# Log-sum-exp over 16384 rows: sixteen loads cut inside the rows, and the last row's raw test ahead of the last range check

## The chip, the core, the metric

One core of a Trainium2 chip runs one program. The metric is device time in microseconds (us) of that core. Most runs of one program agree within 0.3%. "Faster" or "slower" needs 2%, which is 3.3 us here.

## The reference

```python
x = randn(32, 512, 1024).astype(float32)          # 16384 rows of 1024
max_x = max(x, axis=-1, keepdims=True)
out = max_x.squeeze(-1) + log(sum(exp(x - max_x), axis=-1))
```

## The kernel before

The 16384 rows lie over 128 partitions, 128 rows each ("row" below means one row in each of the 128 partitions, 512 KB in all). The kernel doesn't subtract the maximum. It takes exp of the raw data on ScalarE, sums on VectorE or in ScalarE's accumulator, takes the logarithm, and then checks that all sums lie within safe bounds; if any doesn't, a second, safe pass is run under a branch. So the fast path ends twice: with the landing of the last store, and with the branch that skips the second pass.

The rows come in loads into a ring of 48 slots. Each load is worked in pieces. "R" is one exp and one reduce over s rows; "T" is one exp and, per row, one VectorE instruction that adds its two halves with an accumulator; "A" is one exp with ScalarE's own accumulator, for one row.

```python
RING = 48
loads = [
    "R6 R5 R5", "R6 R5 R5", "R8 R8", "R8 R4 R4", "R4 R4 R3 R3 A A", "R6 T3 A A A", "R6 A A",
    "R2 A A T2", "R3 R3", "R3", "A A A", "T2 A", "T2", "T2", "T1", "A", "A",
]
...
    dma = nc.sync.dma_start(out=ring[:, p : p + size, :], in_=source(c, size)).ins
    for how, s in ops:
        v = ring[:, p : p + s, :]
        if how == "A":   exp = nc.scalar.activation(out=o, in_=v, func=AF.Exp, accum_out=sums)
        else:            exp = nc.scalar.activation(out=v, in_=v, func=AF.Exp)
        ...
    if c == LATE:        # 118 rows done: early Ln of 112 rows, early range check
        ...
nc.scalar.activation(out=res[:, W:NC], in_=sumexp[:, W:NC], func=AF.Ln)      # the last 16 rows
nc.sync.dma_start(out=out_rows, in_=res[:, 0:W])
last_store = nc.sync.dma_start(out=out_rest, in_=res[:, W:NC]).ins

check(LATE, LAST, 1)                                       # range check of rows 118 to 126
nc.vector.reduce_max(out=bad[:, 3:4], in_=last_row[:, 0, 0 : d // 16], axis=AX.X)   # raw test,
nc.vector.tensor_scalar(out=bad[:, 2:3], in0=bad[:, 3:4], scalar1=LOG_LOW, ...)     # last row
nc.tensor.matmul(count, lhsT=bad[:, 2:3], rhs=far, start=False, stop=False)
nc.tensor.matmul(count, lhsT=sumexp[:, LAST:NC], rhs=ones, start=False, stop=True)
nc.vector.tensor_scalar(out=fine, in0=count, scalar1=HIGH, scalar2=None, op0=ALU.is_lt)
...                                                        # branch on `fine`
```

`check` is two VectorE instructions (clamp; count what the clamp changed) and a matmul. "Truth value" below means the last instruction shown, `fine`. The "raw test" asks in each partition whether the largest of the first 64 raw values of the last row lies below `LOG_LOW` (the sum could then be too small); it needs the loaded row only, not its exp.

## Time and profile before

| | before |
|---|---|
| time | 163.57 us, median of 3 runs (163.52 to 163.73) |
| span in the trace | 161.76 us |
| busy share of the load queue | 97.0% |
| VectorE, ScalarE busy | 73%, 72% |
| first load landed, last load landed | 21.79, 157.95 |
| last exp, last store issued, landed | 157.98, 159.40, 160.99 |
| truth value; end of SyncE's waits other than for the store | 159.40; 160.55 |

The prediction shows the page's slices, the timeline of ScalarE's waits and the tail, and reads them. Landing times to two decimals are the semaphore events in the trace; where a fence can show them, they are ScalarE's start less 0.02.

### The profile page before, as it was taken

The numbers are of one execution on the slowest core, as the hardware profiler recorded it, in microseconds if no ns is written. First come the engines' busy times: TensorE is split into PE (matmuls) and PEld (weight loads), VectorE is DVE, ScalarE is ACT, GpSimd is POOL, SyncE is SP. The second block draws the span as 40 slices with busy tenths as digits, with TensorE's granted clock in tenths as the row PEclk, the third lists the DMA queues.
The fourth block names the chain that finished last, engine by engine and source line by source line (L and its number), as shares of the span: only waits on it lengthen the run. The fifth ranks groups of instructions, "written<-read, shape, count | busy, mean of one in ns | idle before, by whom it ended". The sixth has DMA issues, their size and how long they took to land.

```text
span 161.8 us, 221 instructions
## 1 busy us (share of the span) xinstructions
PE 0.8 (0%) x8; PEld 0.3 (0%) x8; DVE 118.5 (73%) x56; ACT 117.2 (72%) x60; POOL 0.2 (0%) x4
## 2 busy tenths in 40 slices
PE   0000000000000000000000000000000000000001
PEld 0000000000000000000000000000000000000000
DVE  0000002999959997299995999999999589799772
ACT  3000069980899609994299924999999999999994
POOL 0000000000000000000000000000000000000000
DMA  7996996997997997998898899889999999999990
GB/s 259 519 519 276 502 519 292 486 519 324 454 519 324 454 519 340 438 519 389 389 519 389 389 519 389 389 389 502 405 389 434 474 389 432 416 428 415 418 368 6
DMA packets 2738, 67.19 MB, mean 415 GB/s; under 512 B 560, under 2 KB 560, under 8 KB 944
## 3 DMA queue, kind: packets, MB, share of 16 engines
q1 hardware_dynamic: 2736, 67.18, 97.0%
q14 instruction: 2, 0.02, 0.0%
HBM read 67.11 MB, written 0.07 MB: 415 GB/s over the span
## 4 chain that ended last, share of the span: by engine, by line
DMA 53%; DVE 35%; ACT 10%; issue 1%; PE 0%
DMA ring<-in_x_dram 53%; DVE sumexp L132 35%; ACT ring L122 9%; ACT ring L120 1%; ACT last_exp L120 0%; PE count L202 0%; DVE fine L203 0%
## 5 line engine op out<-in xcount | busy, mean ns | idle before, releaser
L132 DVE TENSOR_REDUCE sumexp<-ring 128x3 f32<-128x3072 f32 (+5 forms) x21 | 109.5, 5276 | 37.2 <-ACT ring L122 37.2
L122 ACT ACTIVATE ring<-ring 128x3072 f32<-128x3072 f32 (+6 forms) x27 | 100.3, 3763 | 41.4 <-DMA ring<-in_x_dram 41.3
L120 ACT ACTIVATE ring<-ring 128x1024 f32<-128x1024 f32 x14 | 14.6, 1040 | 0.0
L137 DVE SCALAR_TENSOR_TENSOR ring<-ring 128x512 f32<-128x512 f32 x12 | 7.7, 687 | 2.1 <-ACT ring L122 2.1
L120 ACT ACTIVATION_READ_ACCUMULATOR ring<-ring 128x1 f32 x14 | 2.6, 187 | 0.0
L75 ACT ACT_TABLE_LOAD x1 | 1.3, 1283 | 0.8 <-PEq L264 0.8
L102 PE MATMUL count<-far,bad 128*1 128x1 f32 x4 | 0.4, 164 | 158.3 <-DVE clamped L98 158.3
L120 ACT ACTIVATE last_exp<-ring 128x1024 f32<-128x1024 f32 x1 | 1.0, 1027 | 0.0
L137 DVE DVE_READ_ACCUMULATOR ring<-ring 128x1 f32 x12 | 1.0, 83 | 0.0
L76 DVE MEMSET ones<- 128x1 f32 x1 | 0.1, 59 | 0.9 <-PEq L264 0.9
L203 DVE TENSOR_SCALAR fine<-count 1x1 int32<-1x1 f32 x1 | 0.1, 145 | 0.6 <-PE count L202 0.6
L94 DVE TENSOR_SCALAR clamped<-sumexp 128x118 f32<-128x118 f32 (+1 forms) x2 | 0.4, 197 | 0.2
L102 PEld LDWEIGHTS count<-far,bad 128*1 128x1 f32 x4 | 0.2, 81 | 158.4 <-DVE clamped L98 158.4
L98 DVE SCALAR_TENSOR_TENSOR clamped<-clamped,sumexp 128x118 f32<-128x118 f32 (+1 forms) x2 | 0.5, 225 | 0.1
L155 ACT ACTIVATE res<-sumexp 128x112 f32<-128x112 f32 x1 | 0.3, 280 | 0.0
L190 ACT ACTIVATE res<-sumexp 128x16 f32<-128x16 f32 x1 | 0.2, 216 | 0.0
L197 DVE TENSOR_REDUCE bad<-ring 128x1 f32<-128x64 f32 x1 | 0.2, 220 | 0.0
L201 PE MATMUL count<-far,bad 128*1 128x1 f32 x2 | 0.2, 164 | 0.2 <-DVE bad L198 0.2
L202 PE MATMUL count<-ones,sumexp 128*1 128x1 f32 x2 | 0.2, 164 | 0.1
L120 ACT ACTIVATION_READ_ACCUMULATOR last_exp<-ring 128x1 f32 x1 | 0.2, 187 | 0.0
L198 DVE TENSOR_SCALAR bad<-bad 128x1 f32<-128x1 f32 x1 | 0.2, 154 | 0.0
L98 DVE DVE_READ_ACCUMULATOR clamped<-clamped,sumexp 128x1 f32 x2 | 0.2, 82 | 0.0
(7 smaller groups left out, 0.6 us busy)
## 6 DMA issues: line engine op xcount, KB each, us to landing
ring<-in_x_dram SPq DMA_DIRECT2D x1, 6144.0 KB, 28.8
ring<-in_x_dram SPq DMA_DIRECT2D x2, 3072.0 KB, 27.9
ring<-in_x_dram SPq DMA_DIRECT2D x3, 1536.0 KB, 29.2
ring<-in_x_dram SPq DMA_DIRECT2D x1, 4096.0 KB, 27.8
ring<-in_x_dram SPq DMA_DIRECT2D x2, 1024.0 KB, 30.0
ring<-in_x_dram SPq DMA_DIRECT2D x3, 512.0 KB, 25.9
ring<-in_x_dram SPq DMA_DIRECT2D x5, 35.3
out_dram<-res SPq DMA_DIRECT2D x1, 56.0 KB, 8.7
```

The source lines that it names most:

```text
L75: nc.scalar.preload_act_table_set("natural_log_exp_and_others")
L94: nc.vector.tensor_scalar(out=clamped[:, c0:c1], in0=sumexp[:, c0:c1], scalar1=LOW, scalar2=HIGH, op0=ALU.max, op1=ALU.min,)
L98: counted = nc.vector.scalar_tensor_tensor(out=clamped[:, c0:c1], in0=clamped[:, c0:c1], scalar=0.0, in1=sumexp[:, c0:c1], op0=ALU.bypass, ...
L102: nc.tensor.matmul(count, lhsT=bad[:, i : i + 1], rhs=far, start=i == 0, stop=False)
L120: exp = nc.scalar.activation(out=o, in_=v, func=AF.Exp, accum_out=sums)
L122: exp = nc.scalar.activation(out=v, in_=v, func=AF.Exp)
L132: added = [nc.vector.reduce_sum(out=sums, in_=v, axis=AX.X)]
L137: nc.vector.scalar_tensor_tensor(out=lo, in0=lo, scalar=1.0, in1=ring[:, p + r, H:d], op0=ALU.mult, op1=ALU.add, accum_out=sums[:, r : r + 1],
L155: ln = nc.scalar.activation(out=res[:, 0:W], in_=sumexp[:, 0:W], func=AF.Ln)
L190: nc.scalar.activation(out=res[:, W:NC], in_=sumexp[:, W:NC], func=AF.Ln)
L197: nc.vector.reduce_max(out=bad[:, 3:4], in_=last_row[:, 0, 0 : d // 16], axis=AX.X)
L198: nc.vector.tensor_scalar(out=bad[:, 2:3], in0=bad[:, 3:4], scalar1=LOG_LOW, scalar2=None, op0=ALU.is_lt)
```

## The change

Its intent: one load fewer, and late loads sized so that ScalarE keeps up with them, by letting a load end inside a row (13.5, 12.5, 7.5, 5.5, 3.5, 2.75, 2.25, 1.5 rows; exp takes what has landed, the sums only whole rows). On VectorE, the raw test of the last row moves ahead of the last range check. Core of the diff (the ring becomes two-dimensional and positions are counted in elements; that and the second pass are cut):

```diff
+    x_rows = x_flat[0 : P * W].rearrange("(p c) d -> p (c d)", p=P)
     loads = [
-        "R6 R5 R5", "R6 R5 R5", "R8 R8", "R8 R4 R4", "R4 R4 R3 R3 A A", "R6 T3 A A A", "R6 A A",
-        "R2 A A T2", "R3 R3", "R3", "A A A", "T2 A", "T2", "T2", "T1", "A", "A",
+        (16, "R8 R7 A"), (16, "R8 R7 T1"), (16, "R8 R8"), (16, "R6 R5 R5"), (13.5, "R5 R4 T4"),
+        (12.5, "R7 R6"), (9, "A A A A A A A A A"), (7.5, "R3 R2 R2"), (5.5, "R4 T2"),
+        (4, "A A A A"), (3.5, "T3"), (2.75, "T3"), (2.25, "T2"), (1.5, "T2"), (1, "A"), (1, "A"),
     ]
-    LATE = 118
+    LATE = 119
...
+                upto = end if k + 1 == len(ops) else p + s * d
+                v = ring[:, here:upto]
                 exp = nc.scalar.activation(out=v, in_=v, func=AF.Exp)
...
-    check(LATE, LAST, 1)
-    nc.vector.reduce_max(out=bad[:, 3:4], in_=last_row[:, 0, 0 : d // 16], axis=AX.X)
-    nc.vector.tensor_scalar(
+    seen = nc.vector.reduce_max(out=bad[:, 3:4], in_=last_row[:, 0 : d // 16], axis=AX.X)
+    low = nc.vector.tensor_scalar(
         out=bad[:, 2:3], in0=bad[:, 3:4], scalar1=LOG_LOW, scalar2=None, op0=ALU.is_lt
     )
+    first, _ = check(LATE, LAST, 1)
+    in_this_order(add, seen)
+    in_this_order(low, first)
```

## The prediction

> **What bounds the kernel now.** I read the page's DMA slices first, then the chain of waits, then the timeline of the last 5 us, and last the landing events of the loads.
>
> The slices of the page (40 of 4.04 us each; busy tenths of the DMA engines, then GB/s) and its queue table:
>
> ```profile
> DMA  7996996997997997998898899889999999999990
> ...
> q1 hardware_dynamic: 2736, 67.18, 97.0%
> ```
>
> The load queue holds 97.0% of 16 engines' span, and the only weak slices are the first and the last. (The sixes and sevens in between are big packets counted whole in the slice where they start.) The input is 67.11 MB, every byte of it is read once before and after, and no slice in the middle is empty: transfers bound this kernel, and the time is one start, one stream, one tail.
>
> The list of ScalarE's waits in the timeline gives the pace of the stream, because ScalarE stands idle until each of the early loads lands (start us, us busy, engine, line; in brackets the idle time before and what ended it):
>
> ```profile
> 21.81 14.04 ACT L122 ACTIVATE ring<-ring 128x6144 f32<-128x6144 f32 x3 [19.74 <-DMA ring<-in_x_dram]
> ...
> 41.15 14.04 ACT L122 ACTIVATE ring<-ring 128x6144 f32<-128x6144 f32 x3 [5.30 <-DMA ring<-in_x_dram]
> ...
> 60.50 13.95 ACT L122 ACTIVATE ring<-ring 128x8192 f32<-128x8192 f32 x2 [5.31 <-DMA ring<-in_x_dram]
> ...
> 79.86 14.04 ACT L122 ACTIVATE ring<-ring 128x8192 f32<-128x8192 f32 x3 [5.41 <-DMA ring<-in_x_dram]
> ...
> 99.21 12.43 ACT L122 ACTIVATE ring<-ring 128x4096 f32<-128x4096 f32 x4 [5.31 <-DMA ring<-in_x_dram]
> ...
> 138.08 8.07 ACT L122 ACTIVATE ring<-ring 128x3072 f32<-128x3072 f32 x3 [0.28 <-DMA ring<-in_x_dram]
> ```
>
> A load of 16 rows per partition (64 KB each) takes 19.34 to 19.36 us. From 99.21 to 138.08, 32 rows came in four loads (12, 8, 6, 6) in 38.87 us; two loads of 16 would take 38.70. Two more loads cost 0.17, so a load costs about 0.08 by itself and a row about 1.204. The landing events confirm it: loads of 12, 8, 6, 3, 2 and 1 rows are 14.53, 9.72, 7.31, 3.69, 2.49 and 1.28 us apart, which 0.079 + 1.2045 per row gives within 0.01. The last row lands at 157.95 (the page: issued at 138.07, landed 19.9 later).
>
> The tail, from the timeline of the last 5 us:
>
> ```profile
> 156.88 1.04 ACT L120 ACTIVATE ring<-ring 128x1024 f32<-128x1024 f32 x1
> 157.29 0.08 DVE L137 DVE_READ_ACCUMULATOR ring<-ring 128x1 f32 x1
> 157.29 0.69 DVE L137 SCALAR_TENSOR_TENSOR ring<-ring 128x512 f32<-128x512 f32 x1
> 157.83 0.19 ACT L120 ACTIVATION_READ_ACCUMULATOR ring<-ring 128x1 f32 x1
> 157.90 0.08 DVE L137 DVE_READ_ACCUMULATOR ring<-ring 128x1 f32 x1
> 157.98 1.03 ACT L120 ACTIVATE last_exp<-ring 128x1024 f32<-128x1024 f32 x1
> 158.09 0.17 DVE L94 TENSOR_SCALAR clamped<-sumexp 128x9 f32<-128x9 f32 x1
> ...
> 159.16 0.22 ACT L190 ACTIVATE res<-sumexp 128x16 f32<-128x16 f32 x1
> ...
> 159.40 0.34 SPq L192 DMA_DIRECT2D out_dram<-res  x1
> 159.40 0.14 DVE L203 TENSOR_SCALAR fine<-count 1x1 int32<-1x1 f32 x1 [0.59 <-PE count L202]
> ```
>
> The last exp starts at 157.98. Elsewhere the next exp follows the start of an accumulator read after 0.09, so ScalarE was ready at 157.83 + 0.09 = 157.92: it waited 0.06, for the landing at 157.95 and the 0.02 to 0.03 that every release takes here. So the load sets the end, but ScalarE is only 0.06 behind; the chain of waits, which sees no gap worth counting, puts that step down to ScalarE. From the last exp the rest is a fixed tail: 0.96 to the accumulator read, 0.22 to the Ln, 0.24 to the store's issue, 1.59 to its landing (160.99), 0.77 of closing barriers to 161.76. The timed value is 163.57, the span 161.8.
>
> **What the Trainium skill says.** "DMA: Bandwidth & Descriptors", Queues, rings and completion order: on each engine descriptors are consumed in ring order. The trace agrees: loads land in order, evenly, with up to eight queued, so a fixed completion cost is hidden except for the last load. The same page, Anatomy of one DMA, puts a fixed cost of about 2.0 us on a DMA issued by another path; here, in a full queue, the trace shows 0.08. The same page, How a descriptor splits into AXI transactions: a descriptor that doesn't start on a multiple of 256 B costs extra beats. The new loads start and end on quarter rows, multiples of 1024 B, so none should; no run before shows it for such sizes. "ScalarE: Activation LUTs", What ACT_TABLE_LOAD costs: 186 ns + 0.833 per element, consecutive instructions overlapping by 93 ns. The trace agrees: 1040 ns for 1024 elements, 7025 for 8192, pairs overlapping by 96.
>
> **The change part by part.** *Removed:* one load (17 to 16), 0.079 us of the stream. *Moved:* the cuts. The first four loads stay 16 rows, so the first landing (21.79) and the pace to 79.84 stay. Bytes are the same. With 0.079 + 1.2045 n, landings after 79.84 are: 13.5 rows 96.18, 12.5 at 111.31, 9 at 122.23, 7.5 at 131.35, 5.5 at 138.05, 4 at 142.95, 3.5 at 147.24, 2.75 at 150.63, 2.25 at 153.42, 1.5 at 155.31, 1 at 156.59, 1 at 157.87. That is 157.95 - 0.08.
>
> *Is the queue still fed?* A load of the second lap may go out when the slots it overwrites have been summed. VectorE needs 140 + 1068 ns per row for a reduce (3345 at 3 rows, 8682 at 8). The first load's sums end at about 45.0, the second's at 65, the third's at 84.8, the fourth's at 102.5, the 13.5-row load's at 114.7, the 12.5-row load's at 131.1. The stream needs load 4 queued by about 58, load 5 by 77, load 6 by 94, load 7 by 109, load 8 (slots of the fourth and the fifth: 108) by 120, load 12 (slots of the sixth: 124.6) by 145. More than 10 us to spare each time: nothing starves.
>
> *ScalarE at the end.* Step from start to start: 0.09 + 0.855 per row, and 1.037 for a row with its accumulator read. From the landing at 122.23: nine such rows to 131.58; 7.5 rows in three pieces to 138.26; 5.5 in two to 143.14; four rows to 147.29; 3.5 rows to 150.37 and the early Ln (0.19) to 150.56. It then waits for the landings at 150.63 (done 153.09) and 153.42 (start 153.44): 2.25 rows to 155.45, 1.5 to 156.83, a row to 157.86. The last row is released at 157.89. ScalarE is ready 0.03 before: again a near tie, 0.09 earlier than now.
>
> *VectorE.* The last pair sum follows the 1.5-row exp, which ends about 156.92: two rows of 0.615 to 158.17. The raw test (steps 0.25 and 0.20) needs only the loaded row, then the range check (0.21, and 0.23 to the PE) ends at about 159.05. The PE still takes the range check's matmul first, in program order, so the three products end at about 159.5 instead of 159.38 and the truth value comes at about 159.57 instead of 159.40. That isn't on the path: the last store lands at about 160.9, and the branch's end, which SyncE saw at 160.37 before, may come at 160.5 unnoticed. The swap is worth 0.
>
> Sum: 0.079 less for the load, 0 for the cuts while their rates hold, 0 for the swap: 163.57 - 0.08 = 163.49.
>
> **The rivals.** (1) Sizes that aren't whole rows cost the transfers something. Eight loads have such sizes, and an engine carries 8 packets of each (128 partitions over 16 engines). With 20 ns more per packet, my guess of a bad case, that is 8 x 8 x 0.02 = 1.3 us: 164.8. Against it: packets have followed size in a straight line so far (161 ns at 4 KB, 912 at 24 KB, 2415 at 64 KB). (2) ScalarE becomes the bound of the tail. Its slack is 0.03, and after the landing at 153.42 it has 4.42 us of work for 4.45 of stream. If each of four steps takes 0.03 more, the end slips 0.1: 163.6. For it: it stands next to the bound already. Against: all durations are measured. (3) The check outlasts the store, through VectorE starting its tests at 158.17 and the PE's order. It would need some 0.4 us more than I find; then 163.6 to 163.8. (4) What looks like ScalarE in the chain of waits is the bound, and the freed backlog gains: at most the 0.06 of waiting turned round, so nothing beyond 0.1 either: 163.45.
>
> **Range and chances.** The three runs before spread over 0.21 (163.52 to 163.73), more than the effect. I take 0.25 either side of 163.5, a bit more than that spread: 163.25 to 163.75. 2% is 3.3 us; a gain of that size would need the stream to be 2% faster at the same bytes, and no term reaches it; a loss needs rival (1) at more than twice the bad case. Faster 0.01, same 0.98, slower 0.01.
>
> **What would show each step.** Right: 16 loads whose landings fit 0.079 + 1.2045 per row, also at 2.75 and 1.5 rows; last landing near 157.87; last exp within 0.05 of it; the same 3.78 from the last exp to the end; the truth value at 159.5 to 159.6, later than before, with no effect. Wrong: packets of 1.5 to 3.5 rows off the straight line; an accumulator read less than 0.1 before the last exp and well after the landing (ScalarE binds); SyncE's last wait ended by the branch and not by the store; a gap in the DMA slices (a starved queue).

## The result, and the profile after

163.47 us, median of 6 runs (163.38 to 163.68), against 163.60 for the kernel before (6 runs, 163.52 to 163.73). The ratio is 0.9994, 95% interval 0.9981 to 1.0007. Predicted: 163.49, range 163.25 to 163.75.

The page's slices and load queue after the change:

```profile
DMA  8995996996996997998899999996999899999990
...
q1 hardware_dynamic: 2592, 67.18, 97.1%
```

The stream is as full as before, with 144 packets fewer: 128 of the missing load, and 16 semaphore writes.

ScalarE's waits in the timeline of the changed kernel (start us, us busy; in brackets the idle time and what ended it):

```profile
21.89 13.09 ACT L137 ACTIVATE ring<-ring 128x8192 f32<-128x8192 f32 x2 [19.81 <-DMA ring<-in_x_dram]
...
79.95 14.04 ACT L137 ACTIVATE ring<-ring 128x6144 f32<-128x6144 f32 x3 [5.41 <-DMA ring<-in_x_dram]
...
96.29 11.91 ACT L137 ACTIVATE ring<-ring 128x5120 f32<-128x5120 f32 x3 [2.30 <-DMA ring<-in_x_dram]
...
111.42 10.96 ACT L137 ACTIVATE ring<-ring 128x6656 f32<-128x6656 f32 x2 [3.23 <-DMA ring<-in_x_dram]
```

The 13.5 rows came 16.34 after the fourth load and the 12.5 rows 15.13 later: the 16.34 and 15.135 of the prediction. The form 128x6656, six and a half rows in one exp, is a piece that starts inside a row; it costs what its size says.

The tail of the changed kernel, from the timeline of its last 5 us:

```profile
157.90 0.19 ACT L132 ACTIVATION_READ_ACCUMULATOR ring<-ring 128x1 f32 x1
157.99 1.01 ACT L132 ACTIVATE last_exp<-ring 128x1024 f32<-128x1024 f32 x1
158.31 0.08 DVE L154 DVE_READ_ACCUMULATOR ring<-ring 128x1 f32 x1
158.49 0.22 DVE L214 TENSOR_REDUCE bad<-ring 128x1 f32<-128x64 f32 x1
158.74 0.15 DVE L215 TENSOR_SCALAR bad<-bad 128x1 f32<-128x1 f32 x1
158.81 0.16 DVE L100 TENSOR_SCALAR clamped<-sumexp 128x8 f32<-128x8 f32 x1
...
159.40 0.34 SPq L210 DMA_DIRECT2D out_dram<-res  x1
159.57 0.14 DVE L223 TENSOR_SCALAR fine<-count 1x1 int32<-1x1 f32 x1 [0.38 <-PE count L222]
```

Three things are to be read here. The last exp now starts 0.09 after the last accumulator read, so ScalarE is the last to be ready, by 0.02 (the load landed at 157.95). VectorE's last sum ends 0.4 later than before (158.39 against 157.99), so its tests start later. And the truth value comes at 159.57, after the store has been issued; before it came with it.

SyncE's own waits at the end say how close the two finishers are. In the profile before:

```profile
SPq L275 <- DVEq L208: 0.5, 1, 0.5
SPq L275 <- DMA out_dram<-res: 0.4, 1, 0.4
```

SyncE waits for VectorE's branch, and then 0.4 more for the store. In the same view of the changed kernel the second line is gone, the wait being too short to be listed (its last other wait ends at 160.72, the store lands at 160.82), and the first has grown:

```profile
SPq L296 <- DVEq L228: 0.6, 1, 0.6
```

One profile against one: the step from the first landing to the last is 136.09 instead of 136.16, and the last store landed 1.42 after its issue instead of 1.59, while the first landing came 0.07 later. So in this pair the 0.17 of the span came from the store's landing, not from the stream. That is what the experiments had to sort out.

### The profile page after: what moved, and what is told of

It reads as the page before. It is cut to its first block, busy times and chain, and to the rows that moved or that the text cites. A ratio compares the mean times of both kernels' runs of the same rounds, so it can differ in the third digit from the quotient of the medians.

```text
span 161.6 us, 227 instructions
## 1 busy us (share of the span) xinstructions
PE 0.5 (0%) x8; PEld 0.3 (0%) x8; DVE 115.0 (71%) x62; ACT 117.0 (72%) x59; POOL 0.2 (0%) x4
## 3 DMA queue, kind: packets, MB, share of 16 engines
q1 hardware_dynamic: 2592, 67.18, 97.1%
## 4 chain that ended last, share of the span: by engine, by line
DMA 59%; ACT 19%; DVE 17%; another core or an unknown queue 3%; issue 1%; SPq 0%; PE 0%
DMA ring<-in_x_dram 59%; ACT ring L137 19%; DVE sumexp L149 15%; DVE ring L154 1%; SPq L120 0%; DVE bad L214 0%; PE count L108 0%; DVE clamped L104 0%; DVE bad L215 0%; DVE fine L223 0%; DVE clamped L100 0%; PE count L222 0%; PE count L221 0%
## 5 line engine op out<-in xcount | busy, mean ns | idle before, releaser
L149 DVE TENSOR_REDUCE sumexp<-ring 128x8 f32<-128x8192 f32 (+6 forms) x17 | 102.9, 6107 | 39.7 <-ACT ring L137 39.7
L137 ACT ACTIVATE ring<-ring 128x8192 f32<-128x8192 f32 (+14 forms) x24 | 98.9, 4175 | 41.5 <-DMA ring<-in_x_dram 41.5
L132 ACT ACTIVATE ring<-ring 128x1024 f32<-128x1024 f32 x15 | 15.6, 1043 | 0.0
L154 DVE SCALAR_TENSOR_TENSOR ring<-ring 128x512 f32<-128x512 f32 x17 | 10.9, 687 | 3.5 <-ACT ring L137 3.5
L104 DVE SCALAR_TENSOR_TENSOR clamped<-clamped,sumexp 128x119 f32<-128x119 f32 (+1 forms) x2 | 0.5, 226 | 0.1
```

Source lines behind the costliest of these rows:

```text
L104: counted = nc.vector.scalar_tensor_tensor(out=clamped[:, c0:c1], in0=clamped[:, c0:c1], scalar=0.0, in1=sumexp[:, c0:c1], op0=ALU.bypass, ...
L149: added = [nc.vector.reduce_sum(out=sums, in_=rows, axis=AX.X)]
L154: nc.vector.scalar_tensor_tensor(out=lo, in0=lo, scalar=1.0, in1=rows[:, r, H:d], op0=ALU.mult, op1=ALU.add, accum_out=sums[:, r : r + 1],)
```

## The experiments

All kernels gave correct results. Each call had its own chip; kernels of one call shared it and the runs of the kernel before. The table has the points of the tail, all from the traces (ScalarE ready: start of the last accumulator read plus 0.09; other waits: the end of SyncE's last wait that isn't for the store; from the store's landing to the end 0.77 passed wherever the store came last; in e7 and e8, where the other waits came last, 0.80 passed from those). e10 is left out of it, since its first load has 4 rows.

| profile | first landing | to last landing | ScalarE ready | last exp | store issued | landed | other waits | span |
|---|---|---|---|---|---|---|---|---|
| before | 21.79 | 136.16 | 157.92 | 157.98 | 159.40 | 160.99 | 160.55 | 161.76 |
| changed | 21.86 | 136.09 | 157.99 | 157.99 | 159.40 | 160.82 | 160.72 | 161.59 |
| e1, changed | 21.88 | 136.04 | 157.98 | 157.98 | 159.39 | 160.88 | 160.69 | 161.65 |
| e5, changed | 21.82 | 136.09 | 157.96 | 157.96 | 159.36 | 160.97 | 160.68 | 161.75 |
| e2, whole rows | 21.92 | 136.01 | 158.29 | 158.29 | 159.70 | 161.11 | 160.85 | 161.88 |
| e4, other sizes | 21.96 | 136.02 | 158.29 | 158.29 | 159.70 | 161.20 | 160.93 | 161.97 |
| e3, old order | 21.96 | 136.00 | 158.02 | 158.02 | 159.43 | 161.30 | 161.14 | 162.07 |
| e6, old order | 21.84 | 136.01 | 157.89 | 157.90 | 159.30 | 161.10 | 161.01 | 161.87 |
| e7, old cuts, new order | 21.90 | 136.22 | 158.09 | 158.15 | 159.57 | 160.99 | 161.13 | 161.93 |
| e8, long raw test | 21.80 | 136.05 | 157.91 | 157.91 | 159.31 | 160.79 | 161.60 | 162.40 |
| e9, old order, shifted | 21.99 | 136.57 | 158.55 | 158.59 | 160.01 | 161.42 | 161.25 | 162.19 |
| e11, fifteen loads | 21.86 | 135.96 | 159.82 | 159.83 | 161.23 | 162.64 | 162.38 | 163.41 |
| e12, odd cuts | 21.87 | 136.03 | 157.95 | 157.96 | 159.36 | 160.77 | 160.67 | 161.54 |

### e1 and e5: the changed kernel again

No edit.

> The changed kernel once more, unedited, to see how far its 0.08 us stands out of the noise. Theory S (the stream of loads sets the end, one load fewer is worth 0.079): 163.5, ratio to before about 0.9995. The step from the first landing to the last should again be 136.09 (it was 136.16 before the change). Rival N (the 0.13 between the medians is the first landing and the last store's landing scattering): the same time, but the first landing moves by some 0.05 to 0.1 and the last store's time to landing (1.59 before, 1.42 after) by 0.1 to 0.2 between profiles of one and the same program.

> The changed kernel a third time, as the partner on this chip of the next three. Both theories: ratio to before between 0.998 and 1.000. The last landing 0.07 to 0.09 after the first landing's step of 136.09; the last store's time to landing anywhere from 1.42 to 1.6.

Measured: e1 163.40 (6 runs) against 163.67, ratio 0.9983 (0.9968 to 0.9997); e5 163.37 (5 runs) against 163.61, ratio 0.9981 (0.9967 to 0.9995). The changed kernel's mean is 0.10, 0.28 and 0.28 below that of the kernel before, so the gain is more likely 0.2 than the predicted 0.08; the 2% is far off in all three. e1's ratio lies a little below what I expected. The first step holds: the stream took 136.04 and 136.09. Rival N holds too: in three profiles of one program the first landing lies between 21.82 and 21.88, and the last store takes 1.42, 1.49 and 1.61. A single pair of profiles can't show a gain of 0.1.

### e2: whole rows

```diff
-(13.5, ...), (12.5, ...), (9, ...), (7.5, ...), (5.5, ...), (4, ...), (3.5, ...), (2.75, ...), (2.25, ...), (1.5, ...),
+(13, ...), (13, ...), (9, ...), (7, ...), (6, ...), (4, ...), (3, ...), (3, ...), (2, ...), (2, ...),
```

> Sixteen loads as in the change, but every cut at a row's end (13, 13, 9, 7, 6, 4, 3, 3, 2, 2, 1, 1 in place of 13.5 to 1.5). Theory S+A (packets cost by size alone, ScalarE stands just behind the stream at the end): last landing unmoved at 157.95; the last two-row load lands at 155.42 and leaves ScalarE 1.80 + 1.04 of work, so it is ready at 158.28 and not at 157.97: 0.3 slower than the changed kernel, 163.8. Rival P (broken rows cost the transfers something): the last landing comes earlier than 157.95 and the time falls below 163.47. Rival Z (the cuts don't matter): 163.5.

Measured: 163.62 (6 runs), ratio to before 0.9994 (0.9981 to 1.0008), 0.22 above e1. The profile has the mechanism where it was expected, in the timeline of e2:

```profile
155.44 1.91 ACT L137 ACTIVATE ring<-ring 128x2048 f32<-128x2048 f32 x1 [0.24 <-DMA ring<-in_x_dram]
...
157.25 1.04 ACT L132 ACTIVATE ring<-ring 128x1024 f32<-128x1024 f32 x1
...
158.29 1.01 ACT L132 ACTIVATE last_exp<-ring 128x1024 f32<-128x1024 f32 x1
```

ScalarE stands idle until two rows land, and they and the next row keep it busy until 158.29, 0.36 after the last landing (157.93). The stream itself took 136.01, against 136.04 to 136.09 with broken rows, so breaking rows cost the transfers at most 0.08. So the fractions aren't there for the transfers, they let ScalarE finish with one load fewer. Without them the one load would have gained next to nothing.

### e3 and e6: the new cuts with the old order of the tests

```diff
+    _, ranged = check(LATE, LAST, 1)
     seen = nc.vector.reduce_max(...)
     low = nc.vector.tensor_scalar(...)
-    first, _ = check(LATE, LAST, 1)
-    in_this_order(add, seen)
-    in_this_order(low, first)
+    in_this_order(ranged, seen)
```

> The changed kernel with the range check ahead of the raw test again, as before the change. Theory: the check isn't on the path, 163.5; the truth value within 0.1 of 159.57, since VectorE starts its tests at 158.4 in either order and does the same work. Rival: the order was worth something: 163.6 or more, with the truth value later and the SyncE's last wait ended by the branch.

> The new cuts with the old order of the tests, once more, since the first try was 0.3 slower than the changed kernel against my expectation, and its VectorE stood 0.52 idle ahead of the range check. Theory C (the check is a second finisher just behind the store: with the new cuts VectorE's last sums end 0.4 later than before the change, and the old order then puts the truth value at about 160.0): 0.2 to 0.3 slower than the changed kernel of this call, the truth value at 159.9 to 160.0 and the idle time there again. Rival L (one bad store landing of 1.87 and scatter): within 0.1 of the changed kernel.

Measured: e3 163.70 (6 runs), ratio 0.9999 (0.9985 to 1.0013), 0.30 above e1; e6 163.58 (5 runs), ratio 0.9994 (0.9980 to 1.0008), 0.21 above e5. I had expected nothing of e3; e6 is the size that theory C gave. The timeline of e6:

```profile
158.21 0.08 DVE L154 DVE_READ_ACCUMULATOR ring<-ring 128x1 f32 x1
158.81 0.17 DVE L100 TENSOR_SCALAR clamped<-sumexp 128x8 f32<-128x8 f32 x1 [0.52 <-DVE ring L154]
...
159.87 0.14 DVE L222 TENSOR_SCALAR fine<-count 1x1 int32<-1x1 f32 x1 [0.33 <-PE count L221]
```

Between the last sum and the range check VectorE stands idle for 0.52, although both semaphores it waits for had arrived (the events lie at 158.30 and earlier). It was 519 ns in e3 and in e6, on two chips. In the trace VectorE's sequencer ends a semaphore instruction at 158.35 and the next instruction starts 0.46 later. In the changed kernel the same 0.46 lies between a semaphore instruction that ends at 158.03 and the raw test at 158.49, but the last sum runs until 158.39 meanwhile, so only 0.10 of it is idle. The new order hides a pause that the old order exposes. The truth value comes 0.3 to 0.5 later in the old order, SyncE's other waits end at 161.01 to 161.14 instead of 160.7, and they pass where the store used to land. But they are not what ends these two profiles: the store's own landing is late as well (1.87 and 1.80 after its issue) and comes last, at 161.30 and 161.10. SyncE's own waits in e3 show both:

```profile
SPq L295 <- DVEq L227: 1.0, 1, 1.0
...
SPq L295 <- DMA out_dram<-res: 0.2, 1, 0.2
```

Without the late store the other waits would still hold the end back to 161.14 (e3) and 161.01 (e6), against landings of 160.82 to 160.97 in the three profiles of the changed kernel. What each of the two late finishers costs over all runs isn't separated.

The landing events say which part of the store is late. It counts as landed when its semaphore has been raised 16 times. In all fourteen profiles the fifteenth comes 1.38 to 1.45 after the issue; only the sixteenth is ever later. How late it is goes with the second of two 8 KB packets that the trace's instruction queue carries near the end (more of them under e9). That packet starts 0.49 and 0.41 after the store's issue in e3 and e6 (landing after 1.87 and 1.80), 0.36 in e5 (1.61), 0.20 in the kernel before and in e4 (1.59, 1.49), and less than 0.1 after it, or not near it, in the other nine (1.41 to 1.49). No run moves that packet alone, so this is a fit and not a test.

### e4: other sizes for three late loads

```diff
-(2.75, "T3"), (2.25, "T2"), (1.5, "T2"),
+(3.25, "T3"), (2, "T2"), (1.25, "T2"),
```

> The changed kernel with 3.25, 2 and 1.25 rows in place of 2.75, 2.25 and 1.5: same loads, same last landing (157.95), but after the landing before the last two single rows ScalarE has less to do. Theory S: ScalarE is ready at about 157.85 instead of 157.99 and now waits for the landing; the last exp starts at 157.97, a gain of 0.02: 163.45. Rival A (ScalarE is the bound of the tail): a gain of 0.1 or more, 163.35.

Measured: 163.75 (6 runs), ratio 1.0003 (0.9988 to 1.0018), 0.35 above e1. A miss of mine: I looked only from the 2-row landing on. The 3.25 rows land at 151.39, ScalarE stands idle 0.55 before them (its wait in the timeline reads 151.41, 5.94 busy, three pieces), and then has 5.85 + 1.04 of work to the last exp where the stream has 6.59. The last exp starts at 158.29 instead of 157.98. It was meant to relieve ScalarE and loaded it; as a test it says the same as e2: the end moves with ScalarE (last exp 0.31 later, time 0.35), while the stream (136.02) stays.

### e7: the old cuts with the new order

The kernel before, with the new order of the two tests and nothing else.

> The kernel before with the new order of the tests alone. Theory C: here VectorE's last sum ends at 157.98, in time for both tests in either order, the truth value stays at 159.4 behind the last matmul, and the time stays that of before: 163.6, ratio 1.000. Rival O (the order is worth 0.2 to 0.3 by itself): 163.35, ratio 0.998.

Measured: 163.66 (5 runs) against 163.61, ratio 1.0000 (0.9987 to 1.0014). By itself the order shows no gain, though the interval reaches 0.2 either way; with the new cuts it is worth 0.2 to 0.3 (e3, e6). The truth value came at 159.58, 0.01 after the store's issue, as before. The pause is here too, 0.49 between VectorE's load of the truth value and its first branch, where 0.08 is usual, so SyncE's other waits end at 161.13, behind the store at 160.99. So the cuts, the order and the place of that pause seem to act together; no run takes them apart.

### e8: a raw test of 1 us

```diff
-    seen = nc.vector.reduce_max(out=bad[:, 3:4], in_=last_row[:, 0 : d // 16], axis=AX.X)
+    seen = nc.vector.reduce_max(out=bad[:, 3:4], in_=last_row[:, 0:d], axis=AX.X)
```

> The changed kernel with the raw test over the whole last row in place of a sixteenth: about 1.0 us more on VectorE in the check and nothing else. Theory C (the branch's end, 160.53 in SyncE's waits, is followed by 0.3 of other waits and so stands 0.1 ahead of the store's landing): the truth value at 160.55, the end 0.85 to 0.95 later, 164.35. Rival F (the check is off the path, as the prediction had it, with 0.4 to spare): 0.6 later, 164.05. Rival Z (the check costs nothing): 163.45.

Measured: 164.19 (5 runs), ratio 1.0033 (1.0019 to 1.0046); 0.82 above e5. In the timeline and in SyncE's waits:

```profile
158.38 1.22 DVE L214 TENSOR_REDUCE bad<-ring 128x1 f32<-128x1024 f32 x1
...
160.46 0.15 DVE L223 TENSOR_SCALAR fine<-count 1x1 int32<-1x1 f32 x1 [0.38 <-PE count L222]
```

```profile
SPq L296 <- DVEq L228: 1.6, 1, 1.6
```

The test grew by 1.00 and the time by 0.82, so the check had about 0.2 to spare. That is nearer to theory C (0.1) than to the 0.4 of my prediction. Here the store (160.79) no longer has a part in the end.

### e9: old order, with three fills more at VectorE's start

```diff
     nc.vector.memset(far, 100 * HIGH)
+    for k in range(3):
+        nc.vector.memset(stats.tile([P, 1], fp32, name=f"spare{k}"), 0.0)
```

> New cuts, old order of the tests, and three idle little fills more at VectorE's start. Theory D (once per run VectorE's sequencer takes 0.46 between one instruction and the next, at a fixed place in its instruction stream, about its 64th record, whatever that instruction is; in the new cuts with the old order this falls on the range check, in the changed kernel it runs beside the last sums): three instructions more move that place onto the last sums, the idle time ahead of the range check shrinks from 519 ns to about 110, the truth value comes at about 159.5, and the time is that of the changed kernel, 163.4, ratio 0.998 to 0.9985. Rival W (the wait belongs to the range check after a sum of two halves, or to the order of the tests): 519 ns again, the truth value at 159.9, 163.6.

Measured: 163.95 (5 runs), ratio 1.0014 (1.0000 to 1.0027). Half of the expectation came out and the time didn't. The idle time ahead of the range check shrank to 107 ns, as theory D says: the pause doesn't belong to that instruction. But the stream took 136.57, half a microsecond more. The queues in the window from 154 to 155 us of e9:

```profile
q1 hardware_dynamic: 93, 0.39, 97.0%
q14 instruction: 1, 0.01, 2.1%
```

In the same window of the changed kernel there is no second line. One packet of 8 KB on the instruction queue started at 154.60 and took 0.33; the load of 1.5 rows, which was in flight, landed 2.50 after the one before it instead of 1.89, and ScalarE waited for it, in the timeline of e9:

```profile
156.12 1.48 ACT L139 ACTIVATE ring<-ring 128x1536 f32<-128x1536 f32 x1 [0.38 <-DMA ring<-in_x_dram]
```

The landing events show one of the load's 16 shares held up: fifteen of its 16 increments had come by 155.47 (all 16 by 155.41 in the changed kernel), and the last at 156.10; in the two loads after it the last increment stays 0.58 behind the fifteenth, too. In the kernel before and the changed kernel two such packets start between 159.07 and 159.60, behind the stream. With three idle instructions more, one of them came forward into it. Where the pause went, e9 doesn't show: no gap of 0.46 is left between VectorE's late instructions. It fits that these packets bring instructions and that the pause has to do with the same supply, but no run separates that; and "about the 64th record" isn't shown, since e9's packet came earlier than three records would make it.

### e10: the first 64 rows in loads of four

```diff
-(16, "R8 R7 A"), (16, "R8 R7 T1"), (16, "R8 R8"), (16, "R6 R5 R5"),
+(4, "R4"), (4, "R4"), (4, "R4"), (4, "R3 A"), (4, "R4"), (4, "R4"), (4, "R4"), (4, "R3 T1"), (4, "R4") x 8,
```

> The changed kernel with each of the first four loads of 16 rows cut into four of 4: twelve loads more, the same bytes, the same end. Theory S (a load costs 0.079 of the stream by itself): the last landing 12 x 0.079 = 0.95 later, 158.9; 164.35, ratio to before about 1.0045. Rival H (with the queue full, the number of loads doesn't matter): 163.4.

Measured: 164.60 (4 runs) against 163.68, ratio 1.0058 (1.0042 to 1.0073). The loads of four are 4.90 apart, as 0.079 + 4 x 1.2045 gives. The 64th row landed at 80.68 instead of 79.92: 0.76 for twelve loads more, of which the first three cost 0.08 together and the other nine 0.68, or 0.076 each. The last landing is at 159.20, not 158.9: between two late loads, 3.36 passed instead of 2.79. A packet of the instruction queue lies in this stretch too (it starts at 152.28), and again only the last of the load's 16 increments is late (154.81 after 154.24). The window of e10 from 148 to 158 has two such packets:

```profile
q14 instruction: 2, 0.02, 0.4%
```

### e11: one load fewer still

```diff
-(2.25, "T2"), (1.5, "T2"),
+(3.75, "T3 A"),
```

> One load fewer still: the 2.25 and the 1.5 rows as one load of 3.75. The sum of my prediction alone (0.079 a load) says 163.3. Theory A (after a landing, ScalarE's remaining work must fit before the last landing): the 3.75 rows land at 155.33, ScalarE then has 2.44 + 1.04 + 1.04 of work, is ready at 159.87 against a last landing of 157.85, and the end moves by 1.9: 165.3, ratio 1.010.

Measured: 165.24 (4 runs), ratio 1.0096 (1.0081 to 1.0112). The timeline:

```profile
155.29 2.55 ACT L137 ACTIVATE ring<-ring 128x2816 f32<-128x2816 f32 x1 [2.05 <-DMA ring<-in_x_dram]
...
159.83 1.00 ACT L132 ACTIVATE last_exp<-ring 128x1024 f32<-128x1024 f32 x1
```

The stream is shorter by 0.08 to 0.13 than in the three profiles of the changed kernel (135.96), and the kernel slower by 1.6 against its own before: ScalarE stands idle for 2.05 while 3.75 rows come in, and can't make it up. This is the limit to which the change went.

### e12: cuts that aren't multiples of 256 bytes

```diff
-(13.5, ...), (12.5, ...), (7.5, ...), (5.5, ...), (3.5, ...), (1.5, ...),
+(13.5 + 8/1024, ...), (12.5 - 8/1024, ...), (7.5 + 8/1024, ...), (5.5 - 8/1024, ...), (3.5 + 8/1024, ...), (1.5 - 8/1024, ...),
```

> The changed kernel with five of its cuts 8 elements (32 bytes) further, so that five loads start off a multiple of 256 bytes. If an unaligned start costs a packet one more transaction of 256 bytes (about 9 ns at the pace of 150 ns for 4096 bytes), 8 packets an engine and load make 0.075 a load, 0.38 in all: the step from the first to the last landing 136.4, time 163.8. If not: 136.05 and 163.4.

Measured: 163.33 (5 runs), ratio 0.9980 (0.9966 to 0.9993); the stream took 136.03. Nothing is lost. (The 256 bytes of the expectation come from the passage of the Trainium skill that the prediction names; the 0.38 was an estimate.) In its packet records a packet of 6112 B took 238 ns where the changed kernel's of 6144 B took 236, and 11264 B from an unaligned start 427 as from an aligned one.

None of the variants beats the changed kernel; e12's 163.33 against 163.37 to 163.47 is noise.

## Why the prediction was right, and where not

**The bound and the stream: right.** 97.1% of the queue, and a landing line of 0.079 per load and 1.2045 per row that held at every new size (packets of 1.5, 2.25, 2.75 and 3.5 rows took 236, 352, 427 and 540 ns; the line through 161 at one row and 2415 at 16 gives 236, 349, 424 and 537). One load fewer took 0.07 from the step between first and last landing in the first pair, 0.07 to 0.16 over all profiles of sixteen loads that have no stray packet, against the 136.16 of before; e7, the other profile of seventeen loads, took 136.22. Rival (1), the cost of broken rows, is refuted by e2 and e12: 1.3 was its size, 0.08 is the most that e2 leaves.

**ScalarE's near tie: right in mechanism, with the sign turned.** The prediction had it ready 0.03 ahead of the last release; it was ready last, by about 0.01 to 0.05. Part of the turn is the last row, which landed 1.25 to 1.26 after the row before it, where the table has 1.28. Of ScalarE's steps, the 2.25 and the 1.5 rows took 3.40 from start to start instead of 3.39, and the landing at 153.42 and everything after it came some 0.1 later than the table had it, most of it because the first landing was 21.86 and not 21.79. e2, e4 and e11 show that the end follows ScalarE one for one when it is late.

**The order of the tests: the step that failed.** "The swap is worth 0" fits the old cuts (e7, within 0.2) and not the new ones: there the old order costs 0.2 to 0.3 (e3, e6). The times of the truth value (159.57) and of the branch (160.53) came out as predicted, in part by luck, since two errors cancel: VectorE's last sum ended at 158.39 and not at 158.17, so that the range check reached the PE at 159.24 and not at 159.05, and from there the three products took 0.30 and not 0.45. And the prediction took the 0.4 between branch and store as slack; e8 has it at 0.2, since SyncE goes through 0.19 of further waits after the branch. It also knew nothing of the pause of 0.46 on VectorE, of which the trace of before shows no idle time. The swap does not shorten the kernel before; with the new cuts, where VectorE's sums end 0.4 later, it keeps that from costing something.

**The tail: not fixed.** "The same 3.78 from the last exp to the end" was 3.60, 3.67 and 3.79 in three profiles of the changed kernel; the store's landing scatters by 0.2, in one of its 16 increments (see e3 and e6).

**The sum.** 0.08 was predicted, the means give 0.10, 0.28 and 0.28. The stream explains about 0.1. That the median of the first call, 163.47, lies 0.02 from the forecast is luck: the other two calls give 163.40 and 163.37. What makes the rest, if it isn't scatter, stays open: only one profile of the unedited kernel before exists, and in it the tail isn't longer than in e5. One reading of the prediction is off a little, without consequence: pairs of exps overlap by 92 to 94 ns, not 96.

## What to carry to other kernels

When a stream of loads sets the end, size the last loads by the engine behind it: after each landing, the work that is left for that engine must fit into what is left of the stream, and a load may end inside a row if that makes it fit. Count every finisher of the program (store, branch, check) with its slack, because a change that is free alone can need the slack that another change used up. A gain of 0.1 in 160 needs repeated profiles of one program first: two of its terms here, the first landing and the store's landing, scatter by as much.

## What the Trainium skill lacked or had wrong

- "DMA: Bandwidth & Descriptors", How a descriptor splits into AXI transactions: it says that a descriptor off a 256-byte start costs extra beats. My estimate from it, in e12, was 0.38 us; nothing was seen: the step from first to last landing 136.03 against 136.04 to 136.09, 11264-byte packets 427 ns either way. It may be hidden at this packet size; the page doesn't say from what size on it matters.
- The same page, Anatomy of one DMA: the fixed cost of about 2.0 us is for one DMA by another path. It has no figure for a DMA in a full queue; here a load adds 0.076 to 0.079 us to the stream (e10, and the landings before).
- The same page, Queues, rings and completion order: it names row 14 as internal to the runtime, refills among its uses, and says that an engine takes turns between rows. The runs don't show the turns, but give a number that the page lacks: with one 8 KB packet of the trace's instruction queue (queue 14) in the middle of the stream, a load landed 0.61 (e9) and 0.57 (e10) late, though the packet took 0.33 and 0.31, and only one of the load's 16 increments was late.
- No page that I read has a pause of 0.46 us of VectorE's sequencer (0.46 in the changed kernel, e3, e6 and e8, 0.49 in all against a usual 0.08 in e7). It may belong to "Runtime: NRT & Kernel Launch", Instruction fetch mechanics, which gives no length for such a pause and says nothing of loads or stores in flight being delayed (0.61 in e9; up to 0.46 between the fifteenth and sixteenth increment of the last store, in e3).
